# A 64-row product of the indexer done over all 128 rows, in a hybrid decoder layer on one core

## The chip, the cores and the metric

The kernel runs on one core of a Trainium2 chip (trn2). The metric is device time in microseconds (us) of one launch; lower is better. Before the change three runs took 848.56, 848.81 and 847.74 us, with a median of 848.56 us.

## What is computed

One decoder layer over 512 tokens of width 1024: a normalisation, one large projection, three mixers (gated linear attention, or GLA; sparse attention; cross-attention into 256 memory tokens), gates, an output projection and a residual. The change lies in the indexer of the sparse attention, which scores every key for every query; the 128 best keys of a query are then kept. Cut to that:

```python
# iq: 8 heads of 64 per query, ik: one key vector of 64 per token, iw: 8 weights per query
s = jax.nn.relu(jnp.einsum('bqhd,bsd->bqhs', iqb.astype(jnp.float32), ik_f))
score = jnp.einsum('bqhs,bqh->bqs', s, iwb.astype(jnp.float32))
score = jnp.where(visible[None], score, -jnp.inf)
_, idx = lax.top_k(score, topk)
```

## The kernel before

Each float32 factor of a product is split into a high and a low part in the format fp32r, and a product of two such factors is made of three: high by high, high by low, low by high (`mm3`, lines 108 to 110). Nearly all of the work is a row of "units". A unit takes one chunk of weights (512 KB, already split) and issues 24 products in four quarters of six, mostly with 128 stationary columns and 512 moving columns. Names such as `gqk0.0`, `gz0.1` or `gv1.0` are units, and in the trace they are the names of the PSUM tiles that the products fill.

The order on every engine is the one in which the program is written out; no scheduler changes it. After each quarter the functions entered for that slot by `at(...)` run, and what they issue stands on TensorE between two quarters. The weights are split ahead of use, two units early, on ScalarE (line 95, `whi`) and VectorE (line 99, `wlo`).

The indexer's query tiles `iqs` (named `iqe` and `iqo` in the trace, for even and odd heads) have 128 rows: 64 rows hold the high part of a head's queries and the other 64 hold the low part; which half is which depends on the parity of the head. `ikh` and `ikl` are the high and low parts of the keys, 64 rows each, copied by DMA into the other 64 rows (lines 319 and 320), so both tiles hold 128 rows with the key parts twice. `score(b, h)` (line 407) handles a block of 128 queries `b` (1 to 3) and one head `h` (0 to 7), so it is called 24 times, once in each of 24 consecutive slots from `gqk0.0`, slot 2, to `gv1.0`, slot 1. It issues two products into one PSUM tile `pis`, whose number of moving columns is n = 256, 384 or 512 for b = 1, 2, 3:

- line 413: stationary `iqs[h]`, all 128 rows, moving `ikh`, which gives (high + low of the queries) by high of the keys in one product;
- line 414: stationary the 64 rows of `iqs[h]` that hold the high part, moving the same 64 rows of `ikl`.

Then ScalarE takes the ReLU (line 417, tile `relu`), and VectorE adds it, weighted, to the scores in `maskadd` (lines 419 and 421, `madd` in the trace). `pis` shares a ring of three PSUM tiles ("at") with tiles of the GLA steps that run in the same slots: `pa` (line 562), `kv` and `po` (through lines 108 to 110), and the ring's next user waits until the tile three allocations ago has been read.

Of the kernel before, what the change touches and what calls it, by code (L numbers as in the profile page):

```python
# [57 lines left out]
def trunk(ctx, tc, x, mem, w_in, w_c, w_kv, w_out, w_o, cols, g_pre, g_mem, g_post, w_up, rel, onehot, out):  # L58
    nc = tc.nc
    pe, act, dve, pool, sp = nc.tensor, nc.scalar, nc.vector, nc.gpsimd, nc.sync  # L60
# [12 lines left out]
    def psum(tag, name):  # L73
        return ps.tile([128, 512], F32, name=name, tag=tag, bufs=PSB[tag])
# [4 lines left out]
    def w2(name, dt=F32, n=512):  # L79
        return wk.tile([128, n], dt, name=name, tag="w2", bufs=NW2)  # L80
# [4 lines left out]
    def k2(tag, name, dt=F32, n=512):  # L85
        return keep.tile([128, n], dt, name=name, tag=tag, bufs=8)

    def kv4(name, shape, dt):
        return keep.tile([128] + shape, dt, name=name, tag="kva", bufs=4)
# [17 lines left out]
    def mm3(o, lh, ll, rh, rl, first=True, last=True):  # L107
        pe.matmul(o, lh, rh, start=first, stop=False)  # L108
        pe.matmul(o, lh, rl, start=False, stop=False)  # L109
        pe.matmul(o, ll, rh, start=False, stop=last)  # L110

# [1 line left out]
    chunks, loads = [], []  # L113

    def add_chunks(src, normal, n=2):
# [48 lines left out]
        if now:  # L164
            flush()

# [1 line left out]
    units, slots = [], {}  # L168
    where = {}

    def unit(name, quarter, done):
        where[name] = len(units)
        units.append((quarter, done))
# [2 lines left out]
        slots.setdefault(4 * where[name] + s, []).append((fn, a))  # L176

    def unit_t(name, rhs, done, n=T):
        """Columns of a chunk to partitions, tokens along the free axis."""
        c = len(units)  # L180
        o = []

        def quarter(q):
            if q == 0:
                o.append(psum("mm", name))
            wh, wl = chunks[c][3]
            for k in (2 * q, 2 * q + 1):
                rh, rl = rhs(k)
                mm3(o[0][:, :n], wh[:, k], wl[:, k], rh, rl, k == 0, k == KT - 1)

        unit(name, quarter, lambda: done(o[0]))

    def unit_n(name, first, lhs, tiles, done):
        """Token tiles to partitions, 256 columns of a chunk pair along the free axis."""
        o = []

        def quarter(q):
            if q == 0:
                o.append(psum("mm", name))
            n = len(tiles)  # L200
            if name[:2] == "dv":
                j, half = divmod(q, 2)
                co = o[0][:, 256 * j:256 * j + 256]
                wh, wl = chunks[first + half][3]
                for p in range(3):
                    for k in range(4):
                        ah, al = lhs(4 * half + k, tiles[j])
                        pe.matmul(co, al if p == 1 else ah, (wl if p == 2 else wh)[:, :, k],  # L208
                                  start=half + p + k == 0, stop=(half, p, k) == (1, 2, 3))
                return  # L210
            for i in range(2 * n * q, 2 * n * q + 2 * n):
                j, k = divmod(i, KT)
                wh, wl = chunks[first + k // 4][3]
                ah, al = lhs(k, tiles[j])
                mm3(o[0][:, 256 * j:256 * j + 256], ah, al, wh[:, :, k % 4], wl[:, :, k % 4],
                    k == 0, k == KT - 1)

        unit(name, quarter, lambda: done(o[0]))
# [11 lines left out]
    def win_t(name, done, **kw):  # L230
        add_chunks(w_in[PIDX[name]], False)
        for i in range(2):
            unit_t(f"{name}.{i}", kw.get("rhs", h_rhs), lambda p, i=i: done(i, p), kw.get("n", T))

    def win_n(name, done):
        add_chunks(w_in[PIDX[name]], True)
        first = len(units)
        for i in range(2):
            unit_n(f"{name}.{i}", first, h_lhs, (2 * i, 2 * i + 1), lambda p, i=i: done(i, p))

# [1 line left out]
    ident = const.tile([128, 128], F32)  # L242
    pool.memset(ident, 1.0)
    pool.affine_select(ident, ident, pattern=[[1, 128]], compare_op=OP.is_equal, fill=0.0,
# [51 lines left out]
            high(dst(i)[0], pts[i])  # L296
        return lambda: [low(dst(i)[1], pts[i], dst(i)[0]) for i in range(2)]

# [1 line left out]
    dvh, dvl = kv4("dvh", [4, 256], F32R), kv4("dvl", [4, 256], F32R)  # L300

    def dv_done(i, p):
# [2 lines left out]

    win_n("dv", dv_done)

    # combined tile: ik | a_low | iw | a_low
    R = {}

    def pc_done(p):
# [21 lines left out]
    iw = const.tile([128, 4, 8], F32)  # L333
# [8 lines left out]

    add_chunks(w_c, False, 1)
    unit_t("pc", h_rhs, pc_done)

    GV = {}
# [6 lines left out]

    win_n("gv0", lambda i, p: gv_done(0, i, p))

    # gate logs: log sigmoid, then sums within chunks of 64 tokens
    def gate_log(h):
        if h == 0:
            R["e"] = [kv4("ebig", [2, 512], F32) for _ in range(2)]
            R["m"] = []  # L360
        p = psum("at", "pla")
        pe.matmul(p, uph[:, 128 * h:128 * h + 128], ar, start=True, stop=True)
        e = R["e"][h // 2][:, h % 2]
        act.activation(e, p, AF.Abs, bias=ba[:, h:h + 1])
        m = w2("la_m")
        dve.tensor_scalar(m, p, ba[:, h:h + 1], 0.0, op0=OP.add, op1=OP.min)
        act.activation(e, e, AF.Exp, scale=-1.0)
        R["m"].append(m)
# [16 lines left out]
    for h in range(4):  # L385
        at("gv0.1", h, gate_log, h)

# [1 line left out]
    iqs = []  # L389

    def iq_done(i, p):
# [15 lines left out]
    def score(b, h):  # L407
        n = 128 * (b + 1)
        sc = maskadd[b]
        q0 = 64 * (h % 2)  # L410
        qsl = slice(128 * (b - 1), 128 * b)
        p = psum("at", "pis")
        pe.matmul(p[:, :n], iqs[h][:, qsl], R["ikh"][:, :n], start=True, stop=False)
        pe.matmul(p[:, :n], iqs[h][q0:q0 + 64, qsl], R["ikl"][q0:q0 + 64, :n],  # L414
                  start=False, stop=True)
        r = w2("relu")
        act.activation(r[:, :n], p[:, :n], AF.Relu)  # L417
        if h == 0:
            dve.tensor_scalar(sc, r[:, :n], iw[:, b, 0:1], None, op0=OP.mult)
        else:  # L420
            dve.scalar_tensor_tensor(sc, r[:, :n], iw[:, b, h:h + 1], sc, op0=OP.mult, op1=OP.add)  # L421
        if h == 7:
            pool.affine_select(sc[:, 128 * b:n], sc[:, 128 * b:n], pattern=[[-1, 128]],
                               compare_op=OP.is_ge, fill=FILL, base=0, channel_multiplier=1)
# [14 lines left out]
        for sc in maskadd[1:]:  # L439
            dve.tensor_scalar(sc, sc, -FMAX, -1e30, op0=OP.not_equal, op1=OP.mult)  # L440

# [1 line left out]
    SKEW = 128 * 641  # L443
    bs = dr.tile([8, 640], F32, name="bs")
    bd = dr.tile([8, SKEW], F32, name="bd")
# [10 lines left out]
        sp.dma_start(bd.rearrange("h (p m) -> h p m", m=641)[:, :, 0:640],  # L456
                     bs[:, None, :].to_broadcast([8, 128, 640]))

# [1 line left out]
    acc = [None] * 8  # L460
    yh = [None] * 8
    yl = [None] * 8
# [34 lines left out]
    def out_units(b, jp):  # L497
        add_chunks(w_out[4 * b + jp], False)
        for i in range(2):
            j = 2 * jp + i  # L500
            unit_t(f"out{b}{j}", lambda k: (yh[k], yl[k]), lambda p, j=j: out_done(b, j, p))

# [1 line left out]
    def c8(ap):  # L504
        return ap.rearrange("p (c s) -> p c s", s=64)

# [133 lines left out]
            win_n(f"gv{h}", lambda i, p, h=h: gv_done(h, i, p))  # L640
        z_units(f"gz{h}")

# [1 line left out]
    kh, kl = None, None  # L644
    Q = [dict() for _ in range(4)]

# [111 lines left out]
        win_t(f"dq{hp}", lambda i, p, hp=hp: dq_done(hp, i, p))  # L758
        z_units(f"dz{hp}")

# [1 line left out]
    mh, ml = [], []  # L762

    def mem_load():
# [54 lines left out]
    def mkv_units(h):  # L819
        add_chunks(w_kv[h], False)  # L820
        for i in range(2):
            unit_t(f"mk{h}.{i}", m_rhs, lambda p, i=i: mk_done(h, i, p), M)
        add_chunks(w_kv[4 + h], True)
        first = len(units)
        for i in range(2):
            unit_n(f"mv{h}.{i}", first, m_lhs, (i,), lambda p, i=i: mv_done(h, i, p))
# [71 lines left out]
    out_units(2, 2)  # L898
    out_units(2, 3)

# [1 line left out]
    mg = [None] * 8  # L902

    def merged(j):
# [58 lines left out]
    def split_b(i):  # L963
        split_next([w[:, i].rearrange("p (k m) -> p k m", m=512) for w in F["w"]])

# [1 line left out]
    for i in range(24):  # L967
        at("gqk0.0", 2+i, score, 1 + i // 8, i % 8)
    for h in range(4):
# [43 lines left out]
    for h in range(4):  # L1013
        n = f"mv{h}.0"
# [13 lines left out]
    for i in range(4):  # L1028
        at(f"fin0{i}", 1, split_b, i)

# [1 line left out]
    xts = [[k2("yh", f"x{tt}{i}") for i in range(2)] for tt in range(4)]  # L1032
    xns = [[k2("acc", f"xn{tt}{i}") for i in range(2)] for tt in range(4)]

# [138 lines left out]
def build(arrays):  # L1173
    import concourse.bacc as bacc
    nc = bacc.Bacc("TRN2", target_bir_lowering=False, num_devices=1)
    aps = [nc.dram_tensor(n, v.shape, mybir.dt.from_np(v.dtype), kind="ExternalInput").ap()
           for n, v in arrays.items()]
    out = nc.dram_tensor("out", (T, D), F32, kind="ExternalOutput").ap()
    with tile.TileContext(nc) as tc:
        trunk(tc, *aps, out)  # L1180
    return nc
# [8 lines left out]
```

## Time and profile before

| | before |
|---|---|
| three runs, median (lowest to highest) | 848.56 us (847.74 to 848.81) |
| span of the profiled execution, first to last instruction | 847.3 us |
| TensorE (PE) busy | 834.1 us, 98% of the span, 4340 products |
| weight loads of TensorE (PEld) busy | 707.2 us, 83% |
| VectorE (DVE) / ScalarE (ACT) busy | 472.2 us, 56% / 330.1 us, 39% |
| GpSimd (POOL) busy | 51.3 us, 6% |

The span of the profiled execution is the one time that the profile gives of it; the three timed runs lie 0.4 to 1.5 us above that span. In the profile, a product is an instruction of PE and the load of its stationary operand is one of PEld. Products are pipelined, and the recorded end of one is modelled, so the time that a product takes from the engine is read as the distance from its start to the next start, and not as its recorded duration.

### The profile page before, as it was taken

Reading aid. Unit: us, or ns where it says so; the run is one execution under the profiler, and the core shown is the slowest. Engines: PE = TensorE matmul, PEld = TensorE weight load, DVE = VectorE, ACT = ScalarE, POOL = GpSimd, SP = SyncE. Lnnn points to the kernel's source line nnn. Section 1 sums busy time; section 2 is a strip of 40 time slices with the busy share of each in tenths; the row PEclk is TensorE's granted clock in tenths of the full one; section 3 lists DMA queues with packets and bytes.
Section 4 is the critical chain, followed back from the end, with each engine's and each line's share of the span. In section 5 each row is a group of like instructions: output and inputs, shape, how many; then the busy total and the mean of one; then the engine's idle time right before and its main releaser. Section 6 shows DMA issues by size and latency. Waiting matters only on the chain.

```text
span 847.3 us, 10810 instructions
## 1 busy us (share of the span) xinstructions
PE 834.1 (98%) x4340; PEld 707.2 (83%) x4340; DVE 472.2 (56%) x839; ACT 330.1 (39%) x597; POOL 51.3 (6%) x77
## 2 busy tenths in 40 slices
PE   7999999999999999999999999999999999999997
PEld 6897678889888888888888788889989898888885
DVE  5577666776767544545676643345555454333623
ACT  5575544444342223323444422423434343322320
POOL 2000010100000021011232000000000000000000
PEclk9999999999999999999999999999999999999999
DMA  6333112412122232132122223333222231225402
GB/s 232 115 119 118 50 50 103 171 50 100 51 100 100 99 125 101 50 125 104 71 75 75 76 100 112 112 109 140 100 100 100 100 134 66 100 99 208 165 1 99
DMA packets 17101, 86.93 MB, mean 103 GB/s; under 512 B 2097, under 2 KB 2609, under 8 KB 8474
## 3 DMA queue, kind: packets, MB, share of 16 engines
q1 hardware_dynamic: 16474, 85.18, 28.8%
q10 hardware_dynamic: 576, 1.05, 0.3%
q8 instruction: 34, 0.56, 0.3%
q14 instruction: 17, 0.14, 0.1%
HBM read 83.03 MB, written 4.74 MB: 104 GB/s over the span
## 4 chain that ended last, share of the span: by engine, by line
PE 95%; DVE 2%; issue 1%; DMA 1%; ACT 0%; SPq 0%; POOL 0%; DVEq 0%; POOLq 0%; ACTq 0%
PE out L108 5%; PE out L110 5%; PE out L109 5%; PE pfin L109 2%; PE pfin L108 2%; PE pfin L110 1%; PE pis L414 1%; PE tpp L700 1%; PE dv.0_227 L208 1%; DMA x<-x 1%; PE dv.1_319 L208 1%; PE pa L562 1%; PE xps L294 1%; PE pov L109 1%; PE pov L110 1%
## 5 line engine op out<-in xcount | busy, mean ns | idle before, releaser
L99 DVE TENSOR_TENSOR wlo<-wraw,whi 128x1024 fp32r<-128x1024 f32 x133 | 166.0, 1250 | 78.2 <-ACT whi L95 77.2
L95 ACT ACTIVATE whi<-wraw 128x1024 fp32r<-128x1024 f32 x133 | 138.6, 1052 | 22.6 <-PE out L109 19.8
L108 PE MATMUL out<-yh,whi 128*128 128x512 f32 x192 | 75.3, 392 | 0.0
L110 PE MATMUL out<-yh,wlo 128*128 128x512 f32 x192 | 74.8, 390 | 0.0
L109 PE MATMUL out<-yl,whi 128*128 128x512 f32 x192 | 74.8, 389 | 0.0
L686 ACT ACTIVATE bm<-bm,nm 128x128 f32<-128x128 f32 (+3 forms) x32 | 18.0, 564 | 76.5 <-DVE nm L684 76.5
L670 POOL TENSOR_TENSOR bm<-toe,madd 128x128 f32<-128x128 f32 (+3 forms) x32 | 31.5, 1004 | 195.9 <-DMA toe<-bd 126.0
L110 PEld LDWEIGHTS out<-yh,wlo 128*128 128x128 f32 x192 | 36.0, 188 | 7.6
L108 PEld LDWEIGHTS out<-yh,whi 128*128 128x128 f32 x192 | 36.1, 188 | 7.3
L109 PEld LDWEIGHTS out<-yl,whi 128*128 128x128 f32 x192 | 36.1, 188 | 7.1
L273 POOL TENSOR_TENSOR rstd<-var,mhalf 128x1 f32<-128x1 f32 x10 | 5.5, 553 | 387.8 <-DVE var L931 289.7
L95 ACT ACTIVATE yh<-th 128x512 fp32r<-128x512 f32 x16 | 10.1, 632 | 46.6 <-DVE th L634 27.6
L494 DVE SCALAR_TENSOR_TENSOR gth<-gth,out 128x512 f32<-128x512 f32 x16 | 11.0, 686 | 28.1 <-PE out L110 28.1
L435 DVE MATCH_REPLACE8 madd<-m,madd 128x256 f32<-128x256 f32 (+2 forms) x48 | 25.6, 543 | 0.0
L431 DVE MAX8 m<-madd 128x8 f32<-128x256 f32 (+2 forms) x48 | 23.6, 546 | 0.0
L684 DVE CUSTOM_DVE_ANT_0 bm<-lg,bm 128x128 f32<-128x128 f32 (+3 forms) x32 | 15.5, 485 | 12.6 <-PE lg L110 12.3
L730 DVE TENSOR_TENSOR ydsa<-pov,th 128x128 f32<-128x128 f32 x32 | 7.8, 284 | 22.3 <-PE pov L110 22.3
L421 DVE SCALAR_TENSOR_TENSOR madd<-relu,iw,madd 128x256 f32<-128x256 f32 (+2 forms) x21 | 12.9, 616 | 12.5 <-ACT relu L417 12.4
L95 ACT ACTIVATE pth<-tpp 128x128 fp32r<-128x128 f32 (+3 forms) x32 | 13.7, 428 | 12.7 <-PE tpp L700 12.7
L417 ACT ACTIVATE relu<-pis 128x256 f32<-128x256 f32 (+2 forms) x24 | 11.5, 488 | 16.4 <-PE pis L414 16.2
L99 DVE TENSOR_TENSOR yl<-th,yh 128x512 fp32r<-128x512 f32 x16 | 11.1, 692 | 11.2 <-ACT yh L95 11.2
L928 ACT ACTIVATE sq<-pfin 128x512 f32<-128x512 f32 x8 | 4.8, 598 | 31.4 <-PE pfin L110 31.4
(1026 smaller groups left out, 2365.1 us busy)
## 6 DMA issues: line engine op xcount, KB each, us to landing
wraw<-w_in SPq DMA_DIRECT2D x43, 1024.0 KB, 4.8
wraw<-w_out SPq DMA_DIRECT2D x12, 1024.0 KB, 4.7
wraw<-w_kv SPq DMA_DIRECT2D x8, 1024.0 KB, 4.8
wraw<-w_o SPq DMA_DIRECT2D x4, 1024.0 KB, 4.8
bd<-bs SPq DMA_DIRECT2D x1, 2560.0 KB
x<-x SPq DMA_DIRECT2D x8, 256.0 KB, 6.0
toe<-bd SPq DMA_DIRECT2D x8, 256.0 KB, 5.0
xres<-x SPq DMA_DIRECT2D x4, 512.0 KB, 8.3
```

What stands on the lines that cost most here:

```text
L95: act.activation(hi, src, AF.Copy, scale=scale)
L99: dve.tensor_tensor(lo, src, f(hi), op=OP.subtract)
L108: pe.matmul(o, lh, rh, start=first, stop=False)
L109: pe.matmul(o, lh, rl, start=False, stop=False)
L110: pe.matmul(o, ll, rh, start=False, stop=last)
L208: pe.matmul(co, al if p == 1 else ah, (wl if p == 2 else wh)[:, :, k], start=half + p + k == 0, stop=(half, p, k) == (1, 2, 3))
L421: dve.scalar_tensor_tensor(sc, r[:, :n], iw[:, b, h:h + 1], sc, op0=OP.mult, op1=OP.add)
L431: dve.max(out=M8[b], in_=maskadd[b])
L435: dve.match_replace(out=maskadd[b], in_to_replace=M8[b], in_values=maskadd[b], imm_value=-FMAX)
L670: pool.tensor_tensor(bm[:, :n], Q[hp]["toe"][i][:, 384 - 128 * qb:512], maskadd[qb], op=OP.add)
L684: dve.tensor_tensor_reduce(out=bm[:, :n], in0=lg[:, :n], in1=bm[:, :n], scale=-1.0, scalar=FMAX, op0=OP.add, op1=OP.min, accum_out=nm)
L686: act.activation(bm[:, :n], bm[:, :n], AF.Exp, scale=-1.0, bias=nm, accum_out=su)
```

## The change

The second product of `score` takes all 128 rows of `iqs[h]` and of `ikl`. Since the other 64 rows hold the low part of the queries, it now also adds low by low, a term that was left out before. Nothing else of the program changes (three comments and the variable `q0` go, so that every line number from 409 on is two lower afterwards).

```diff
     def score(b, h):
         n = 128 * (b + 1)
         sc = maskadd[b]
-        q0 = 64 * (h % 2)
         qsl = slice(128 * (b - 1), 128 * b)
         p = psum("at", "pis")
         pe.matmul(p[:, :n], iqs[h][:, qsl], R["ikh"][:, :n], start=True, stop=False)
-        pe.matmul(p[:, :n], iqs[h][q0:q0 + 64, qsl], R["ikl"][q0:q0 + 64, :n],
-                  start=False, stop=True)
+        pe.matmul(p[:, :n], iqs[h][:, qsl], R["ikl"][:, :n], start=False, stop=True)
```

The order of the instructions is the same on every engine. One wait moves: that for the DMA which fills the second half of `ikl`. These are TensorE's first two scores, in the unit `gqk0.0`, with the waits of each product in brackets. Before:

```order
L110 MATMUL gqk0.0_743<-hh,wlo 128x512
L413 MATMUL pis<-ikh,iqe 128x256 [waits DMAHW6_49,DMAHW2_49]
L414 MATMUL pis<-ikl,iqe 128x256
L108 MATMUL gqk0.0_743<-hh,whi 128x512
...
L110 MATMUL gqk0.0_743<-hh,wlo 128x512
L413 MATMUL pis<-ikh,iqo 128x256 [waits DMAHW3_49]
L414 MATMUL pis<-ikl,iqo 128x256 [waits DMAHW7_49]
```

And after:

```order
L110 MATMUL gqk0.0_743<-hh,wlo 128x512
L412 MATMUL pis<-ikh,iqe 128x256 [waits DMAHW6_49,DMAHW2_49]
L413 MATMUL pis<-ikl,iqe 128x256 [waits DMAHW7_49]
L108 MATMUL gqk0.0_743<-hh,whi 128x512
...
L110 MATMUL gqk0.0_743<-hh,wlo 128x512
L412 MATMUL pis<-ikh,iqo 128x256 [waits DMAHW3_49]
L413 MATMUL pis<-ikl,iqo 128x256
```

The wait for the copy of `ikl` moved from the second score's second product to the first score's second product; all other waits are those of before.

## Rows read from the trace of the kernel before

**Rows 1.** The page: busy time by engine, and the chain that ended last.
```profile
PE 834.1 (98%) x4340; PEld 707.2 (83%) x4340; DVE 472.2 (56%) x839; ACT 330.1 (39%) x597; POOL 51.3 (6%) x77
...
PE 95%; DVE 2%; issue 1%; DMA 1%; ACT 0%; SPq 0%; POOL 0%; DVEq 0%; POOLq 0%; ACTq 0%
```

**Rows 2.** Timeline of PE, a 256-column score: start, duration (us), engine, line, tiles, shape.
```profile
67.97 0.39 PE L110 MATMUL gqk0.0_743<-hh,wlo 128*128 128x512 f32 x1
68.20 0.28 PE L413 MATMUL pis<-ikh,iqe 128*128 128x256 f32 x1
68.40 0.38 PE L414 MATMUL pis<-ikl,iqe 64*128 64x256 f32 x1
68.72 0.50 PE L108 MATMUL gqk0.0_743<-hh,whi 128*128 128x512 f32 x1
69.05 0.40 PE L109 MATMUL gqk0.0_743<-hl,whi 128*128 128x512 f32 x1
```

**Rows 3.** Timeline of PE's weight loads around the same score.
```profile
67.97 0.19 PEld L413 LDWEIGHTS pis<-ikh,iqe 128*128 128x128 f32 x1
68.40 0.18 PEld L414 LDWEIGHTS pis<-ikl,iqe 64*128 64x128 f32 x1 [0.24 <-issue]
68.71 0.19 PEld L108 LDWEIGHTS gqk0.0_743<-hh,whi 128*128 128x128 f32 x1
```

**Rows 4.** Waits of the weight loads: who, total us, times, longest.
```profile
PEld pis L414 <- issue: 7.0, 24, 0.4
```

**Rows 5.** Timeline of PE, a 384-column score.
```profile
89.43 0.34 PE L413 MATMUL pis<-ikh,iqo 128*128 128x384 f32 x1
89.70 0.43 PE L414 MATMUL pis<-ikl,iqo 64*128 64x384 f32 x1
90.06 0.50 PE L108 MATMUL gz0.1_946<-hh,whi 128*128 128x512 f32 x1
90.40 0.39 PE L109 MATMUL gz0.1_946<-hl,whi 128*128 128x512 f32 x1
```

**Rows 6.** Timeline of PE, a 512-column score with GLA products behind it.
```profile
105.41 0.39 PE L413 MATMUL pis<-ikh,iqe 128*128 128x512 f32 x1
105.73 0.50 PE L414 MATMUL pis<-ikl,iqe 64*128 64x512 f32 x1
106.16 0.38 PE L108 MATMUL po<-vh,a 128*128 128x256 f32 x1
106.38 0.28 PE L109 MATMUL po<-vl,a 128*128 128x256 f32 x1
```

**Rows 7.** Timeline of PE, from full-array GLA products into a unit.
```profile
101.77 0.28 PE L110 MATMUL kv<-vh,kk 128*128 128x256 f32 x1
101.89 0.40 PE L108 MATMUL gqk1.0_1031<-hh,whi 128*128 128x512 f32 x1
102.12 0.40 PE L109 MATMUL gqk1.0_1031<-hl,whi 128*128 128x512 f32 x1
```

**Rows 8.** Timeline of PE, 384-column products of a unit, all 128 rows.
```profile
59.05 0.33 PE L109 MATMUL iq1.0_659<-hl,whi 128*128 128x384 f32 x1
...
60.26 0.33 PE L110 MATMUL iq1.1_700<-hh,wlo 128*128 128x384 f32 x1
```

**Rows 9.** Busy time of the engines from the first score to the last; then PEclk, DMA.
```profile
68.20:124.53 56.33, 56.33 (x249) 39.46 (x247) 34.71 (x58) 27.95 (x58) 3.76 (x6) 1.00 0.21 75
```

**Rows 10.** Waits of PE's products in the whole span, all but the start.
```profile
PE pov L109 <- DVE ptl L99: 1.7, 2, 1.4
```

**Rows 11.** Timeline, the ring tile `po` between its two uses.
```profile
107.32 0.39 PE L108 MATMUL gqk1.0_1031<-hh,whi 128*128 128x512 f32 x1
...
109.51 0.84 ACT L624 ACTIVATE on<-po,rstd 128x256 f32<-128x256 f32 x2 [1.15 <-POOL rstd L273]
...
111.71 0.38 PE L108 MATMUL po<-vh,a 128*128 128x256 f32 x1
```

**Rows 12.** Timeline of the DMA issues: the copy into the second half of `ikl`.
```profile
35.73 0.46 SPq L320 DMA_DIRECT2D ikl<-ikl x1
```

## The prediction

> **What bounds the kernel now.** I read the page first: busy times and the chain that ended last. TensorE is busy for 834.1 of 847.3 us and makes up 95% of the chain [rows 1]. So a microsecond that TensorE no longer spends counts in full, as long as nobody else becomes late. Then I looked at the stretch in which the 24 scores stand, from 68.20 to 124.53 us: TensorE has no gap in it by the records, VectorE is busy for 34.71 and ScalarE for 27.95 of its 56.33 us, the granted clock is 1.00 (the 2.4 GHz level), and DMA uses 0.21 of its engines [rows 9]. TensorE is the bound there too, though "busy" hides how well it is used. That shows only in the distances between starts, in the timeline.
>
> **What a score costs now.** In the first score, the full-array product of line 413 starts at 68.20, the 64-row product at 68.40, the next unit product at 68.72 and the one after it at 69.05 [rows 2]. The distances are 0.20 (256 columns), 0.32 (256 columns) and 0.33 (512 columns). What such products cost without a 64-row neighbour stands elsewhere: a 256-column product of 128 rows starts 0.12 us before its successor, and a 512-column one 0.23 us before its own, even where the PSUM tile, both operands and the number of columns all change between them [rows 7]. So all three distances are too long: by 0.08, 0.20 and 0.10 us. The 64-row product with its half-filled array is the dearest of the three, and it makes its neighbours on both sides dear.
>
> The weight loads tell why. The load for line 413 starts at 67.97, in the same instant as the product before it, so it is hidden behind that product. The load for the 64-row product starts only at 68.40, together with its own product, after 0.24 us in which the load path stood and waited for nothing that the profile shows; the next full load starts at 68.71, again together with its product [rows 3]. This idle time is there before all 24 of the 64-row loads and adds up to 7.0 us [rows 4]. I read it as a switch between 64 rows and 128 rows in which the pipeline runs empty, once on the way in and once on the way out.
>
> The Trainium skill, TensorEngine Tiling (Array Packing), section Key Properties, says that changing the tiling mode, and not just the tile, drains TensorE. Its section When to Use Tiling speaks the other way, for row tiling where the contraction is at most 64, and so against this change. The rows bear out the first: no second 64-row product stands beside this one for a gain. By the second alone the sum would be zero or a small loss.
>
> **The change part by part.** Each of the 24 second products becomes a full-array product. Its columns, its PSUM tile and its place stay; the stationary operand is again 128 columns, and its load took 0.18 us with 64 rows and takes 0.19 us with 128 [rows 3], on a path that is hidden once it may run ahead. The price without the switch I take from the nearest full-array rows:
>
> - 256 columns (8 scores): now 0.20 + 0.32 + 0.33 = 0.85 up to the second product behind the score [rows 2]; then 0.12 + 0.12 + 0.23 = 0.47 [rows 7]. Saved 0.38 each, 3.0 in all.
> - 384 columns (8 scores): now 0.27 + 0.36 + 0.34 = 0.97 [rows 5]. A full-array 384-column product takes 0.173: seven steps from 59.05 to 60.26 [rows 8]. Then 0.173 + 0.173 + 0.23 = 0.576. Saved 0.39 each, 3.2 in all.
> - 512 columns (8 scores): now 0.32 + 0.43 + 0.22 = 0.97, with a 256-column product behind [rows 6]; then 0.23 + 0.23 + 0.12 = 0.58. Saved 0.39 each, 3.1 in all.
>
> The sum is 9.3 us. That the saving is nearly the same for each width fits a fixed cost per switch and not one per column. What stands behind a score varies: mostly a unit product, three times `kv`, twice `po`, and three times products of another kind (`pa` twice, a transpose once). For these three I take the same 0.39. Reading each distance to 0.01 us, with three of them in each score, leaves about 0.02 per score, or 0.5 us in the sum.
>
> Three things come at no cost. The moved wait for the copy into `ikl`: that DMA was issued at 35.73 us, more than 30 us before the first score [rows 12]. It would cost only if that copy took 30 us. The order on ScalarE, VectorE, GpSimd and the DMA queues does not change, so nothing is queued behind anything new. The extra low-by-low term rides in rows of the array that were empty, and is covered by the columns that stream anyway.
>
> **What is late next.** The stretch shrinks from 56.33 to 47.0 us. VectorE's 34.71 us in it then make 74% and ScalarE's 27.95 us 59%: neither is full. But single chains have a fixed length that does not shrink with TensorE. The tightest I found is the ring tile `po`. Its first use ends on TensorE where the next unit product starts, at 107.32; ScalarE, GpSimd and ScalarE again work on it until 109.51 + 0.84 = 110.35; its ring slot is used again at 111.71 [rows 11]. That leaves 1.36 us to spare. Between the two uses lie one whole score and the two own products of another, whose saving is 0.39 + (0.32 + 0.43 - 0.46) = 0.68 us. So 0.68 us stay, and the tile should still be free in time. I therefore take nothing off. From below, a wait could cost as much as the worst one that products show after the start, 1.4 us, of 1.7 us for two of them together [rows 10]; this is the bound for a chain that I misjudged.
>
> Behind the last score the whole program is only moved earlier. The weight loads are triggered by the splits, which follow TensorE's own order, so they move along.
>
> **The rivals.**
>
> *The load still does not run ahead.* The two products of a score load the same stationary tile one after the other, and the second load could stay exposed: 0.19 us [rows 3] in each score would be left. The gain would be 24 x (0.39 - 0.19) = 4.8 us and the time 843.8 us. Against it: full loads start together with the full-array product before them [rows 2, 3], and lines 108 and 109 load the same `whi` twice in succession at 0.23 us a product [rows 7]. The Trainium skill, TensorE: Matmul & The Clock Gate, section The mechanism, states a rule that would bring it about: a load overlaps with a product in flight only where the row groups differ. The trace disagrees: the full load at 67.97 started in the very instant of a full-array product.
>
> *A wait takes the place of the switch.* A ring tile or an operand comes late, because ScalarE and VectorE have 9 us less for the same work. Two waits of 1 to 1.4 us [rows 10] would give 841.2 to 842.0 us. For it: VectorE at 74%, with splits of weights in its queue. Against it: the 0.68 us that the tightest chain has left.
>
> *The long distances have another cause.* If the second product into the same tile, or the slice of the query tile, were what is slow, nothing would change: 848.6 us. Against it: `kv` and its neighbours change tile and operands freely and cost nothing [rows 7].
>
> *Slower.* The ring of three tiles becomes the bound: the ReLUs on ScalarE fall behind, each score waits for a tile, and TensorE stands at every one of the 24 places. A score takes 56.33 / 24 = 2.35 us of the stretch now [rows 9]; it decides from the point at which ScalarE and VectorE need more than that for each score in a closed round. At 2.5 us a round the price is 24 x 0.15 = 3.6 us and the time 852.2 us. Against it: ScalarE needs 27.95 / 24 = 1.16 and VectorE 34.71 / 24 = 1.45 us of work for each score [rows 9].
>
> **How the numbers follow.** The profiled span goes from 847.3 to 838.0 us. The median of the runs lies 1.26 us above that span; what lies around the span is not touched, so I keep the difference: 848.56 - 9.3 = 839.3 us. The chances are 0.82 for this forecast, 0.08 for a wait in its place, 0.04 for the exposed load, 0.04 for no gain and 0.02 for slower. The forecast's own range is 838.2 to 840.4 (0.5 us of reading and 0.5 us of scatter between runs, as the three show). To hold the waits too, the range goes up to 842.2; below it ends at 837.8, should the three odd neighbours save more than I took. Faster by over 0.2% (about what a measurement of this kernel can tell from no change, 1.7 us) holds the forecast, the waits and the exposed load: 0.94. No change 0.04, slower 0.02.
>
> **What would show it.** In the timeline after, the first score's two products and the unit product behind them should stand 0.12, 0.12 and 0.23 us apart; the second product's load should start with the first product, and the row of 24 idle times before it should be gone. The distance from the first score to the last should be about 9 us less than 56.33, minus what the last one saves behind it. If the distances shrink but the span does not, look for a wait of PE on ScalarE or VectorE between 68 and 140 us, first at `po`. If the distances stay, the row count was not the cause.

## The result

The changed kernel took 839.86 us (median of four runs, 839.60 to 840.41) against 848.68 us for the kernel before: a ratio of 0.9899, 95% interval 0.9887 to 0.9911, and 8.8 us less between the medians. In a second comparison it was 839.45 against 849.06 us, ratio 0.9892 (0.9873 to 0.9911). The forecast was 839.3 us, in a range from 837.8 to 842.2.

The page of the kernel after, in the lines that answer to [rows 1]: TensorE still sets the end; it has lost 9.0 us of busy time, with as many instructions as before. (In the changed kernel the two products of a score stand on lines 412 and 413, one lower than before; from the ReLU on, line numbers are two lower.)

```profile
span 838.7 us, 10810 instructions
PE 825.1 (98%) x4340; PEld 707.8 (84%) x4340; DVE 471.6 (56%) x839; ACT 329.1 (39%) x597; POOL 51.8 (6%) x77
...
PE 93%; DVE 2%; ACT 1%; issue 1%; DMA 1%; POOL 0%; SPq 0%; DVEq 0%; POOLq 0%; ACTq 0%
```

The first score in the timeline of PE (start, duration in us, engine, line, tiles, shape), to be held against [rows 2]:

```profile
68.63 0.39 PE L110 MATMUL gqk0.0_743<-hh,wlo 128*128 128x512 f32 x1
68.85 0.28 PE L412 MATMUL pis<-ikh,iqe 128*128 128x256 f32 x1
68.97 0.28 PE L413 MATMUL pis<-ikl,iqe 128*128 128x256 f32 x1
69.08 0.40 PE L108 MATMUL gqk0.0_743<-hh,whi 128*128 128x512 f32 x1
69.32 0.40 PE L109 MATMUL gqk0.0_743<-hl,whi 128*128 128x512 f32 x1
```

The distances are now 0.12, 0.11 and 0.24 us, where they were 0.20, 0.32 and 0.33. The weight loads of the same place, against [rows 3]:

```profile
68.63 0.19 PEld L412 LDWEIGHTS pis<-ikh,iqe 128*128 128x128 f32 x1
68.86 0.19 PEld L413 LDWEIGHTS pis<-ikl,iqe 128*128 128x128 f32 x1
68.97 0.19 PEld L108 LDWEIGHTS gqk0.0_743<-hh,whi 128*128 128x128 f32 x1
```

Each load now starts with the product ahead of its own: the load for line 413 at 68.86 beside the product of line 412 (68.85). The 24 idle times of [rows 4] are gone from the list of waits. At the wider scores it is the same; these are the 512-column score that answers to [rows 6] (0.23, 0.22 and 0.12 us):

```profile
99.78 0.39 PE L412 MATMUL pis<-ikh,iqe 128*128 128x512 f32 x1
100.01 0.39 PE L413 MATMUL pis<-ikl,iqe 128*128 128x512 f32 x1
100.23 0.28 PE L108 MATMUL po<-vh,a 128*128 128x256 f32 x1
100.35 0.28 PE L109 MATMUL po<-vl,a 128*128 128x256 f32 x1
```

From the start of the first score to the start of the last it was 55.48 us before (68.20 to 123.68) and is 46.70 us now (68.85 to 115.55): 8.78 us less. One wait is new. It stands in the list of waits of the weight loads (who, total us, times, longest):

```profile
PEld po L108 <- ACT on L622: 0.5, 1, 0.5
```

It cost 0.38 us (0.27 in the distance ahead of it, 0.10 behind it). So 23 scores saved 8.78 + 0.38 = 9.16 us, 0.40 each; with the last one's 0.38 that is 9.5 us gross and 9.2 net. The profiled execution shows 8.6 us between the spans, because its first score started 0.65 us later than in the one before. That was lost in the first 22 us, where both programs issue the same: TensorE waited 2.06 us there for a normalised tile against 1.71 us, and some of the first products were slower. The change does not explain it: when the changed kernel was run again, its first score started at 68.20, as before.

### The profile page after: what moved, and what is told of

Its sections match the earlier page's. It is cut to its first block, busy times and chain, and to the rows that moved or that the text cites. A ratio compares the mean times of both kernels' runs of the same rounds, so it can differ in the third digit from the quotient of the medians.

```text
span 838.7 us, 10810 instructions
## 1 busy us (share of the span) xinstructions
PE 825.1 (98%) x4340; PEld 707.8 (84%) x4340; DVE 471.6 (56%) x839; ACT 329.1 (39%) x597; POOL 51.8 (6%) x77
## 4 chain that ended last, share of the span: by engine, by line
PE 93%; DVE 2%; ACT 1%; issue 1%; DMA 1%; POOL 0%; SPq 0%; DVEq 0%; POOLq 0%; ACTq 0%
PE out L110 5%; PE out L108 5%; PE out L109 5%; PE pfin L110 2%; PE pfin L108 2%; PE pfin L109 2%; PE tpp L698 1%; PE dv.0_227 L208 1%; DMA x<-x 1%; PE dv.1_319 L208 1%; PE xps L294 1%; PE pov L109 1%; PE pa L560 1%; PE pov L110 1%; DVE wlo L99 1%
## 5 line engine op out<-in xcount | busy, mean ns | idle before, releaser
L99 DVE TENSOR_TENSOR ptl<-tpp,pth 128x128 fp32r<-128x128 f32 (+3 forms) x32 | 15.4, 483 | 0.0
```

Of the source, the lines that this page charges most:

```text
L99: dve.tensor_tensor(lo, src, f(hi), op=OP.subtract)
```

## The experiments

Every kernel was timed against the kernel before on the same chip. "The changed kernel" is that of the result.

**Both products with 64 rows.** The edit, on the kernel before:

```diff
-        pe.matmul(p[:, :n], iqs[h][:, qsl], R["ikh"][:, :n], start=True, stop=False)
+        pe.matmul(p[:, :n], iqs[h][q0:q0 + 64, qsl], R["ikh"][q0:q0 + 64, :n],
+                  start=True, stop=False)
```

> Both products of a score take 64 rows (the first leaves out low part of the queries by high part of the keys). Theory A, a fixed cost for each change between 64 and 128 rows: there are still two changes per score, so about the time of the kernel before, 848.7 us (847.5 to 850); the dear distances move to the unit product ahead of the score and to the score's last product, and the two 64-row products stand 0.12 us apart at 256 columns. Theory B, each 64-row product is dear in itself by about 0.2 us: 24 more of them, 853 us or more. Theory C, what is dear is two products in a row with different stationary tiles into one PSUM tile: no change of that here, 848.7 us, but the distances stay where they were (0.20, 0.32, 0.33 us).

Measured: 848.28 us, ratio 0.9997 (0.9987 to 1.0006). Twice as many 64-row products cost nothing more, so theory B falls. The timeline of PE at the second score:

```profile
68.72 0.39 PE L110 MATMUL gqk0.0_743<-hh,wlo 128*128 128x512 f32 x1
69.03 0.38 PE L413 MATMUL pis<-ikh,iqo 64*128 64x256 f32 x1
69.25 0.28 PE L415 MATMUL pis<-ikl,iqo 64*128 64x256 f32 x1
69.46 0.50 PE L108 MATMUL gqk0.1_805<-hh,whi 128*128 128x512 f32 x1
69.80 0.39 PE L109 MATMUL gqk0.1_805<-hl,whi 128*128 128x512 f32 x1
```

And its weight loads:

```profile
69.03 0.18 PEld L413 LDWEIGHTS pis<-ikh,iqo 64*128 64x128 f32 x1 [0.36 <-issue]
69.14 0.19 PEld L415 LDWEIGHTS pis<-ikl,iqo 64*128 64x128 f32 x1
69.46 0.19 PEld L108 LDWEIGHTS gqk0.1_805<-hh,whi 128*128 128x128 f32 x1
```

The unit product ahead of the score now takes 0.31 us instead of 0.23: a change stands behind it, where there was none. The two 64-row products take 0.22 and 0.21 instead of 0.12, and the product behind the score 0.34 instead of 0.23. So each change of the row count costs about 0.1 us on the product ahead of it and 0.1 us on the product behind it. In the kernel before, the 64-row product stood between two changes and bore 0.2 us. My expectation that the two 64-row products would stand 0.12 us apart missed this: each still borders on one change. In no run does a 64-row product stand without a change beside it, so that it would then cost 0.12 us, as a full one does, is worked out and not measured. That theory C falls is seen at the first of these distances, which theory C leaves at 0.23.

**Half as many changes: scores in pairs.** Two scores per slot: both products of line 413, then both of line 414. The core of the edit, with pairs of heads in different halves of the array:

```diff
+        ps_ = [psum("at", "pis") for _ in hs]
+        for h, p in zip(hs, ps_):
+            pe.matmul(p[:, :n], iqs[h][:, qsl], R["ikh"][:, :n], start=True, stop=False)
+        for h, p in zip(hs, ps_):
+            q0 = 64 * (h % 2)
+            pe.matmul(p[:, :n], iqs[h][q0:q0 + 64, qsl], R["ikl"][q0:q0 + 64, :n],
+                      start=False, stop=True)
...
-    for i in range(24):
-        at("gqk0.0", 2+i, score, 1 + i // 8, i % 8)
+    for i in range(12):
+        at("gqk0.0", 3 + 2 * i, scores, 1 + i // 4, ((0, 1), (2, 3), (4, 5), (6, 7))[i % 4])
```

> Two scores per slot in 12 slots, 64-row second products back to back, in different halves of the array (even head, odd head). Theory A (cost per change of the row count): half the changes, so half the gain of the change: 844.3 us (843.3 to 845.3). If two 64-row products in different halves also run beside each other, up to 12 x 0.17 = 2 us less, 842.3 us. Theory B (cost per 64-row product): 848.7 us.

The same with pairs in one half, `((0, 2), (1, 3), (4, 6), (5, 7))`:

> As the pairs before, but the two 64-row products back to back use the same half of the array (heads 0 and 2, 1 and 3, and so on). Theory A: 844.3 us (843.3 to 845.3); the difference to the pairs in different halves is what running beside each other is worth, 0 to 2 us. Theory B: 848.7 us.

And, as a control, the pairs with both products over all 128 rows:

> Two scores per slot in 12 slots, all products over 128 rows: the changed kernel with the pairing alone. All theories: 839.9 us, plus 0 to 1 us if ring tiles come late because two scores come at once. It tells what of the pairs' time is the pairing.

| | us | ratio to before (95% interval) |
|---|---|---|
| pairs, 64 rows, different halves | 842.15 | 0.9927 (0.9911 to 0.9944) |
| pairs, 64 rows, same half | 844.64 | 0.9953 (0.9938 to 0.9968) |
| pairs, 128 rows | 840.52 | 0.9906 (0.9891 to 0.9921) |

All three came out as theory A has it. Half the changes, with pairs in the same half, win back 4.0 of 8.8 us. Against the control, the pairs over 128 rows, they cost 4.1 us, or 0.17 for each of their 24 changes. The timeline of PE with pairs in the same half (x2 is two products in one row):

```profile
70.01 0.40 PE L413 MATMUL pis<-ikh,iqe 128*128 128x256 f32 x2
70.33 0.50 PE L416 MATMUL pis<-ikl,iqe 64*128 64x256 f32 x2
70.76 0.50 PE L108 MATMUL gqk0.1_805<-hh,whi 128*128 128x512 f32 x1
```

And in different halves:

```profile
69.23 0.28 PE L413 MATMUL pis<-ikh,iqo 128*128 128x256 f32 x1
69.44 0.38 PE L416 MATMUL pis<-ikl,iqe 64*128 64x256 f32 x1
69.44 0.38 PE L416 MATMUL pis<-ikl,iqo 64*128 64x256 f32 x1
69.75 0.49 PE L108 MATMUL gqk0.1_805<-hh,whi 128*128 128x512 f32 x1
```

In the same half two 64-row products take 0.43 us together, 0.2 of it for the changes. In different halves they start in the same instant and take 0.31 together. Running beside each other is thus worth 0.12 us a pair at 256 columns, and 2.5 us in all by the times. Even so the full-array pairs are 1.6 us faster: their two products take 0.12 us each and pay for no change. The pairing itself costs 0.6 us by the two ratios (0.9906 against 0.9899), which their intervals do not tell from nothing. In the trace of the full-array pairs ScalarE has two ReLUs at once, and two loads of scores wait for a ReLU to free a ring tile, 0.9 us together.

One rival has no measurement: that a product is cheap when all 128 rows enter the sum, however it is cut. The changed kernel with its second product cut into two 64-row products, rows 0 to 63 and 64 to 127, into one PSUM tile would have tested it, but nothing in that program orders the two halves' writes to the tile, and it has no time. The pairs speak against this rival, as the price of the same 24 products of 64 rows fell by half with the number of changes; the cut itself stays untested.

**The price of the product itself.** The second product left out; the scores lack the low part of the keys.

> The changed kernel without the second product of a score at all (low part of the keys left out). It gives the price of a full-array second product: 8 x (0.12 + 0.173 + 0.23) = 4.2 us less than the changed kernel by the distances, 835.5 us (834.7 to 836.6; chains that are late may keep up to 1 us). If the time falls by much more, the full-array product is not as cheap as its distance says; the 64-row one then costs 4.2 + 9.3 = 13.5 us in the kernel before.

Measured: 837.27 us (835.99 to 839.25), ratio 0.9878 (0.9855 to 0.9900). The expectation missed: not 4.2 but about 1.8 us less than the changed kernel, by the two ratios. The distances are as cheap as expected (0.11 us for the first score's one product); but now chains are late at several places. The list of waits of the weight loads:

```profile
PEld po L108 <- ACT on L621: 1.4, 1, 1.4
PEld kv L108 <- DVE S L590: 0.7, 1, 0.7
...
PEld pa L559 <- issue: 0.5, 1, 0.5
PEld pis L412 <- ACT on L621: 0.4, 1, 0.4
```

Summed over the distances at these places, 2.7 us go into waits, of which the changed kernel has 0.4 already (below). So the changed kernel stands just at the point where the rest of this stretch begins to hold TensorE up: of the next 4.2 us to be had there, more than half would be lost.

**The new wait.** In the trace of the changed kernel, around the first use of `po` (engines POOL, ACT, PE and the weight load, in order of time):

```profile
101.31 0.40 PE L108 MATMUL gqk1.0_1031<-hh,whi 128*128 128x512 f32 x1
...
101.92 1.22 POOL L421 TENSOR_SCALAR_AFFINE_SELECT madd<-madd 128x128 f32<-128x128 f32 x1 [18.67 <-DVE madd L419]
...
103.23 0.28 POOL L618 TENSOR_SCALAR gvar<-gss 128x2 f32<-128x2 f32 x1
...
104.34 0.84 ACT L622 ACTIVATE on<-po,rstd 128x256 f32<-128x256 f32 x2 [1.92 <-POOL rstd L273]
...
105.23 0.19 PEld L108 LDWEIGHTS po<-vh,a 128*128 128x128 f32 x1 [0.53 <-ACT on L622]
```

The same two GpSimd instructions in the kernel before:

```profile
105.57 1.22 POOL L423 TENSOR_SCALAR_AFFINE_SELECT madd<-madd 128x128 f32<-128x128 f32 x1 [20.06 <-DVE madd L421]
...
108.45 0.23 POOL L620 TENSOR_SCALAR gvar<-gss 128x2 f32<-128x2 f32 x1 [1.66 <-ACT on L617]
```

Before, GpSimd had finished the causal mask 1.66 us ahead of the norm of `po`. Now the mask runs from 101.92 to 103.14, and the norm, queued behind it, starts at 103.23, although its input was there at 102.42 (the last read of ScalarE's sums). The chain from the end of `po`'s first use to its release grew from 3.03 us (107.32 to 110.35) to 3.87 us (101.31 to 105.18). Of these 0.84 us, 0.72 are the time that the norm stands ready on GpSimd: 0.81 us now (102.42 to 103.23) and 0.09 before (108.36 to 108.45). To test that, the mask of the second block was issued four slots later, behind the second norm:

```diff
-        if h == 7:
-            pool.affine_select(sc[:, 128 * b:n], sc[:, 128 * b:n], pattern=[[-1, 128]],
-                               compare_op=OP.is_ge, fill=FILL, base=0, channel_multiplier=1)
+        if h == 7 and b != 2:
+            causal(b)
...
+    at("gqk0.0", 21, causal, 2)
```

> The changed kernel once more, beside the three that follow: 839.9 us, 8.8 us less than the kernel before on the same chip.

> The changed kernel with GpSimd's causal mask of the second query block four slots later, behind the second po. Theory A (TensorE's one new wait of 0.5 us at po comes from GpSimd, where the mask stands in front of the GLA norm): the wait of po on ScalarE is gone, 839.5 us, 0.4 us less than the changed kernel. Theory B (the chain through ScalarE is too long anyway): the wait stays, 839.9 us.

Measured: 838.90 us with the late mask (ratio 0.9884, 0.9864 to 0.9903) and 839.45 us for the changed kernel beside it (0.9892, 0.9873 to 0.9911). The times are as theory A says, but their intervals overlap; it is the lists of waits that tell them apart, first the changed kernel and then the late mask:

```profile
PEld po L108 <- ACT on L622: 0.6, 1, 0.6
```

```profile
PEld po L108 <- ACT on L626: 0.2, 1, 0.2
```

Most of the wait came from GpSimd's queue; 0.2 us stays, so theory B has a small part too. With the late mask the norm starts 0.09 us after its input again, but the chain still takes 3.53 us (99.16 to 102.69): the norm's two GpSimd instructions last 0.57 and 0.80 us there, and 0.28 and 0.72 in the changed kernel. Why they last longer stays open.

**The same cost in the columns, and a faster kernel.** The GLA's `pa` products change the shape of the array too: line 562 of the kernel before uses 128 by 128, line 564 only 64 columns, in turns. In the changed kernel their lines are 560 and 562, and the timeline of PE behind a score is as follows (x2 is here one product, which the profile records as a pair of passes):

```profile
78.16 0.39 PE L560 MATMUL pa<-qd,kd 128*128 128x128 f32 x2
78.47 0.33 PE L562 MATMUL pa<-qd,kte 128*64 128x64 f32 x2
78.73 0.49 PE L560 MATMUL pa<-qd,kd 128*128 128x128 f32 x2
79.15 0.33 PE L562 MATMUL pa<-qd,kte 128*64 128x64 f32 x2
79.41 0.50 PE L108 MATMUL gz0.0_867<-hh,whi 128*128 128x512 f32 x1
```

The first full-width pair takes 0.31 us, with one change behind it; the second takes 0.42, with a change on either side. So a change to 64 columns ahead of a product costs it 0.1 us, as a change of the rows does: in the kernel before, where the first pair stood behind a 64-row product, it took 0.42 us too (80.77 to 81.19). What the change behind the pair costs is not isolated here, as no such pair stands without one. Both products were therefore made full: the key tile holds even, decayed even and odd chunks side by side, and each product takes 128 columns of it with 64 moving columns. The edit of the products (that of the key tile, with three more VectorE instructions for each of the four heads, is left out here):

```diff
-            pe.matmul(pa[:, s], g["kd"][:, s], qd[:, s], start=True, stop=True,
-                      skip_group_check=True)
-            pe.matmul(pa[0:64, 128 * p + 64:128 * p + 128], g["kte"][:, 64 * p:64 * p + 64],
-                      qd[:, 128 * p + 64:128 * p + 128], start=True, stop=True,
-                      skip_group_check=True)
+            for u in range(2):
+                k0, q0 = 192 * (p % 2) + 64 * u, 128 * p + 64 * u
+                pe.matmul(pa[:, q0:q0 + 64], g["kx"][p // 2][:, k0:k0 + 128], qd[:, q0:q0 + 64],
+                          start=True, stop=True, skip_group_check=True)
```

> The changed kernel with the GLA's pa products, one of them 128 rows by 64 columns of the array, made into two full-array products of 64 moving columns each (the key tiles laid out as even, even decayed, odd; two more small VectorE instructions for each). Theory A (a change of the array's used shape costs, columns as well as rows): 32 changes fewer and the next product 0.1 us earlier; 0.67 us a pair becomes about 0.45, 16 pairs: 3.5 to 5 us less than the changed kernel, 835 to 836.4 us. Theory B (only the row count costs): half of the moving columns are saved in the first product only, 0 to 1.5 us less, 838.4 to 839.9 us.

Measured: 835.95 us, ratio 0.9851 (0.9832 to 0.9870): 3.5 us less than the changed kernel beside it, and 13.1 us less than the kernel before. The timeline of PE:

```profile
78.52 1.00 PE L571 MATMUL pa<-qd,kx 128*128 128x64 f32 x8
79.33 0.47 PE L108 MATMUL gz0.0_870<-hh,whi 128*128 128x512 f32 x1
79.65 0.39 PE L109 MATMUL gz0.0_870<-hl,whi 128*128 128x512 f32 x1
```

A call of `pa` takes 0.81 instead of 1.25 us, and 8 calls make the 3.5 us, more than theory B allows. The unit product behind it still takes 0.32 us instead of 0.23, though no change of shape is left there. Its load is late as well: it starts at 79.31, with its own product (79.33) and not with the one ahead. The same stands behind the wait at `po` in the changed kernel, with no change of shape either: the load starts at 105.23 with its product, which takes 0.22 us where 0.12 is usual. So in these traces the 0.1 us behind goes with a load that did not run ahead, and a change of shape is one thing that holds a load back. What holds it back behind `pa` stays open. The moving columns changed along with the shape, so this run alone does not isolate the change of columns; the distances 0.31 and 0.42 above do, for the change ahead.

> Both of these together. If they are independent their gains add up: 834.6 to 836 us by theory A for pa, 838 to 839.5 us by theory B.

Measured: 836.03 us, ratio 0.9853 (0.9830 to 0.9875). The gains did not add up. The wait at `po` is again down to 0.2 us in the trace, but the time is that of full `pa` alone. Whether the late mask is worth the 0.55 us that lay between the medians above stays open.

## Why the prediction was right, point by point

- **What bounds the kernel.** Right: 9.2 us net taken from TensorE between 68 and 116 us came out as 8.8 and 9.6 us of time in the two comparisons.
- **The sum.** 0.38 to 0.39 us a score were forecast, 0.40 measured; 9.3 against 9.5 us gross. Reading it off the distances between starts in the trace of before was good to 0.2 us. Two small sums are off by 0.1 us: 0.5 and 0.5 us around 839.3 make 838.3 to 840.3, and two waits of 1 to 1.4 us make 841.3 to 842.1; nothing hangs on them.
- **The cause.** The switch between row counts, in and out, was right, and shown by moving the changes (both products with 64 rows) and by halving them (pairs). The detail was wrong: I called the 64-row product itself the dearest. It cost 0.2 us more than a full one because it had a change on either side; with one change it costs 0.1 more. The rule of the Trainium skill, TensorEngine Tiling (Array Packing), Key Properties, that a change of tiling mode drains the engine, agrees with these runs; the price is what they add, 0.2 us a change. The Trainium skill's rule in the same section, that tiles operate independently, agrees with the pairs in different halves, both of which started at 69.44. Neither helps a lone 64-row product between full ones.
- **The load.** The rival in which the second load stays exposed is refuted: it starts at 68.86 beside a full-array product that started at 68.85.
- **What is late next.** The place was right, the verdict wrong. I left the ring tile `po` 0.68 us to spare. What failed is that I took its chain as fixed at 3.03 us; it grew to 3.87 us, mostly because the causal mask, on GpSimd for another chain, came in front of it. The mask came later relative to `po` because the ReLU that feeds it did: it started 2.33 us after its score's products (98.40 to 100.73), where it was 0.47 before (103.91 to 104.38). In both kernels ScalarE has to split a GLA state from VectorE and a chunk of weights ahead of that ReLU. Before, it began on them at 103.11, ahead of the end of the products; now it waited for the state until 99.46, more than 1 us behind it. So the queues of VectorE and ScalarE had fallen behind TensorE here. The rival "a wait takes the place of the switch" thus came true at one place and for 0.38 us, not for the 2 to 3 us that it was priced at. The 0.2 us that the scores saved beyond the forecast made up for half of it, and partly by this luck the net stands at 9.2 us against the 9.3 forecast. The 0.5 us by which the first median lies above the forecast is within what the two comparisons differ by (8.8 and 9.6 us less).
- **Other cause, and slower.** Both are refuted by the first runs: the distances fell to those of full-array rows, and ScalarE and VectorE did not become the bound, though in the run without the second product waits for them took back more than half of the next 4.2 us.

## What to carry to other kernels

A product over part of the array's rows or columns between full ones is not cheaper but dearer: here each change between 64 and 128 rows cost 0.2 us, half on the product ahead and half on the one behind. Where the missing rows or columns can be filled with something harmless or masked, fill them; where they can't, put products of one shape next to each other, in different halves of the rows if possible. The cost is read in the distances between starts and in weight loads that start with their own product instead of the one before, not in the busy share, which is 98% before and after; and when TensorE gets faster, follow what else is queued on each engine of the next chain, not only the length of the chain.

## What was not expected of the hardware

Two 64-row products in different halves of the array and in different PSUM tiles started in the same instant (69.44 us both) and took 0.12 us less than two in the same half. And a full product behind one that uses all 128 rows but only 64 of the columns pays the same 0.1 us as behind one with 64 rows (0.31 and 0.42 us for the same pair of passes with one change and with two).
